# Weight parts lent to GpSimd in the mixing projections, with the turn between two blocks and a routing in another order

## The chip, the cores and the metric

The kernel runs on one core of a Trainium2 chip. A core has a matrix engine (TensorE; in the profile PE, its weight loads PEld), a vector engine (VectorE, DVE), an activation engine (ScalarE, ACT), GpSimd (POOL) and a queue that issues the transfers (SyncE, SP). They run side by side, each takes its own instructions in a fixed order, and semaphores tell one when another is done. The metric is the device time of one execution in microseconds, the median of several.

## The reference

One sequence of 256 tokens with 1024 channels goes through two blocks, all in float32. The first has two layers; in each:

```python
x = x + 0.5 * swiglu_ffn(rms_norm(x, ffn1_norm_g[l]), ffn1_w_in[l], ffn1_w_out[l])
proj = rms_norm(x, mix_norm_g[l]) @ w_mix_in[l]          # 1024 x 3328
...   # 8 heads of a delta-rule recurrence (rwkv7) from 1792 columns, 8 heads of attention from 1536
x = x + concatenate([y_rwkv, y_moba]) @ w_mix_out[l]
x = x + memory_cross_attention(...)                       # 256 tokens of a memory
x = x + 0.5 * swiglu_ffn(...)
```

A norm closes it. The second block computes six rows of modulation from a condition vector `c` (`c @ w_ada + b_ada`: shift, scale and gate, twice), and then:

```python
h = rmsnorm(x, norm1_w) * (1 + scale1) + shift1
proj = h @ w_in            # a chunked mLSTM, a differential attention, gates
x = x + gate1 * (merged @ w_out)
h2 = rmsnorm(x, norm2_w) * (1 + scale2) + shift2
# logits of 4 groups and 32 experts: h2 @ w_rg + b_rg, h2 @ w_re + b_re
# top group, top 2 of its 8 experts; each expert is a swiglu of width 256
x = x + gate2 * sum over experts of combine[:, e] * (silu(h2 @ w_gate[e]) * (h2 @ w_up[e])) @ w_down[e]
```

## The kernel before, in words

**A product.** The weights lie in main memory as units of 128 partitions x 2048 columns, read as two halves of 128 x 1024 (`raw`, 512 KB each). PE multiplies in a reduced float32 form, so each operand is cut into two parts: ACT rounds a half to `wh`, DVE subtracts, `wl = raw - wh` (`parts`, L534). The activations have parts too, `XH` and `XL`. `mm3` (L568) then issues three products into one accumulation in PSUM: `XH wh`, `XH wl`, `XL wh`. A half of a projection of 512 columns has four such triples.

**What is prepared when.** `prefetch` (L556) keeps halves ahead in the order of a fixed stream: in the mixing stage `wh` and `wl` have two buffers each, so the parts of a half are written while the half before it is multiplied; the feed-forward stages lend a third buffer, the second block has five. `raw` has four. A list `behind` names instructions; the parts that are made next are put behind them on their engine (`issue_after`).

**The order of the work.** Each stage is a set of generators (`mix`, `proj`, `rwkv_early`, `lora` and so on). `Weave` picks the next by priority and by due times from a planner of its own (`Clock`, L252), which has costs for every engine's operations, GpSimd's too. The order in which instructions come out is the order of each engine's queue, as far as the framework does not move them.

**The mixing stage** (`mix`, L865) multiplies 13 units a layer: unit 0 the low-rank inputs, 1 to 6 the columns of the recurrence in the order in which the heads need them, 7 to 12 the attention's. Between the products run the heads: DVE builds decays and keys with scans and element-wise operations (`rwkv_early`, L955), PE and DVE solve a triangular system (`rwkv_chunk`, `rwkv_solve`), GpSimd computes powers for the norms and a few products of 256 or 512 columns.

**The turn.** `final_norm` (L1509) waits for the last feed-forward, sums the squares of `x` and of `x` times the gain (ACT, eight calls; DVE multiplies by the gain), and GpSimd computes the power `r`. `block2` (L1939) then calls `prep_modulated` (L733): for each half of the channels DVE scales two token tiles by `rr`, PE transposes them into PSUM, ACT and DVE apply scale and shift, and `split` makes `XH` and `XL`. After the first two scalings two halves of weights are made. `settle` (L1543) scales `x` itself on GpSimd.

**The routing.** `route_weights` (L2035), spawned at lowest priority in the middle of the second block, loads the 288 columns of router weights and the bias, multiplies shift by the weights on PE (eight products) for the bias, and scales and splits the weights. `route` (L2055) multiplies `h2` by them (two accumulating passes in each of eight blocks; the second half waits for the second half of `X`), makes logits, takes the first largest group, counts places with three small products, and `places` makes the permutation with which `pick` gathers the tokens of each expert group.

Of the kernel before, what the change touches and what calls it, by code (L numbers as in the profile page):

```python
# [19 lines left out]
P = 128  # L20
D = 1024
KT = 8
# [425 lines left out]
class Prog:  # L448
    def __init__(self, ctx, tc, a):
        self.clock = Clock()  # L450
        self.tc, self.nc, self.a = tc, Timed(tc.nc, self.clock), a
        nc = self.nc
        pool = lambda name, **k: ctx.enter_context(tc.tile_pool(name=name, **k))
        self.cp = pool("cst", bufs=1)
        self.wp = pool("wts", bufs=2)
        self.ap_ = pool("act", bufs=2)
        self.pp = pool("psum", bufs=2, space=PSUM)
        self.dp = pool("dram", bufs=1, space=DRAM)
        self.uid = 0
        self.turn = {}  # L460
        self.weave = Weave(self.clock)
        self.spawn = self.weave.add
        self.order, self.loads, self.ahead = stream(), collections.deque(), collections.deque()
        self.chunks, self.mod = collections.deque(), None
        self.version, self.uses = [1, 1], 0
        self.sp, self.spare = None, {}
        self.behind, self.stop = [], None
        self.loan = {}

# [4 lines left out]
    def ps(self, tag):  # L474
        n = BANKS[tag]
        return self.tile(self.pp, [P, 512], F32, tag, tag, n)

# [56 lines left out]
    def parts(self, raw):  # L534
        h, l = self.wtile("wh", F32R), self.wtile("wl", F32R)
        with ExitStack() as later:
            for z in self.behind:
                later.enter_context(self.tc.issue_after(z.ins))
            quiet, self.clock.quiet = self.clock.quiet, True
            self.nc.scalar.activation(h, raw, AF.Copy)  # L540
            self.nc.vector.tensor_sub(l, raw, h.bitcast(F32))
            self.clock.quiet = quiet
        return h, l

    def weights(self, name, j, i, n=99):

        self.prefetch(n)
        u, w = self.ahead.popleft()
        assert u == (name, j, i), (u, name, j, i)
        return w  # L550

# [4 lines left out]
    def prefetch(self, n=99):  # L556
        while len(self.ahead) < min(n, self.lookahead("wh")):
# [5 lines left out]
            self.ahead.append((u, self.parts(raw)))  # L563
# [4 lines left out]
    def mm3(self, out, xh, xl, wh, wl, start, stop):  # L568
# [3 lines left out]
        mm(out, xl, wh, start=False, stop=stop)  # L572
# [26 lines left out]
    def setup(self):  # L599
# [31 lines left out]
        self.modc = self.cp.tile([P, 48], F32, name="modc")  # L631
        self.gates = self.dp.tile([2, 8, P], F32, name="gates")

    def setup_later(self):

        yield 0, 12.0
        self.nc.sync.dma_start(self.csts[:, P:], self.a["cst"][:, P:])
        self.setup2()
        yield 0, 20.0
        self.setup_bias()  # L640
# [92 lines left out]
    def prep_modulated(self, gain, shift):  # L733
# [3 lines left out]
        for hf in range(2):  # L737
            xn = []
            for t in range(2):
                xn.append(self.k("s2", 512))  # L740
                z = nc.vector.tensor_scalar(xn[t], self.x[t][:, hf * 512:hf * 512 + 512], self.rr[:, t:t + 1], None, op0=OP.mult)
            if hf == 0:
                self.behind, self.stop = [z, *self.behind], None
                self.prefetch(2)
            for k in range(0, 4, 2):
# [15 lines left out]
                self.behind = self.split(pair.H[:, sl], pair.L[:, sl], tg.rearrange("p (k t) -> p k t", k=2))  # L761
# [747 lines left out]
    def final_norm(self):  # L1509
# [11 lines left out]
        def squares(i, hf):  # L1521
            for t, x in enumerate(self.halves(self.x)):
                j = 4 * i + 2 * hf + t
                sq = nc.scalar.activation(self.k("s2", 512), x[hf], AF.Square, accum_out=ss[:, j:j + 1])
# [18 lines left out]
    def settle(self):  # L1543

        r = self.rsqrt(self.rf, 2, 1.0 / D, EPS)
        for t in range(2):
            self.nc.gpsimd.tensor_scalar(self.x[t], self.x[t], r[:, t:t + 1], None, op0=OP.mult)
# [100 lines left out]
    def modulation(self, l):  # L1648

        sc = self.sp.tile([P, 8], F32, name=f"sc{l}")  # L1650
# [288 lines left out]
    def block2(self):  # L1939
# [4 lines left out]
        self.bident, self.bmask = (self.cst(n).bitcast(BF16) for n in ("bid", "bmask"))  # L1944
        X = yield from self.prep_modulated(*self.modulation(0))
# [89 lines left out]
    def route_weights(self):  # L2035

        nc = self.nc
        self.sc, self.shift = self.modulation(1)
        w = self.k("wrt", 288)
        nc.sync.dma_start(w, self.a["wrt"])  # L2040
        b = self.row("brt", "brt", 36)
        yield 0, self.due(w)
        o = self.ps("tr")
        for k in range(KT):
            nc.tensor.matmul(o[:, :36], self.shift[:, k:k + 1].to_broadcast([P, P]), w[:, k * 36:(k + 1) * 36],
                             start=k == 0, stop=k == KT - 1)
        self.brow = self.sp.tile([P, 36], F32, name="brow")
        nc.vector.tensor_tensor(self.brow, o[:, :36], b, op=OP.add)
        v = w.rearrange("p (k n) -> p k n", n=36)
        nc.vector.tensor_tensor(v, v, self.sc[:, :, None].to_broadcast([P, KT, 36]), op=OP.mult)  # L2050
        self.wr = self.sp.tile([P, KT, 72], F32R, name="wr")
        self.split(self.wr[:, :, :36], self.wr[:, :, 36:], v)
        yield 1.7, 0

    def route(self, X, N):  # L2055
# [6 lines left out]
        for k in range(KT):  # L2062
            if k == 4:
                yield lambda: X.ok[1]
            if k:
# [14 lines left out]
        for t in range(2):  # L2080
            stt(lg[:, t], o[:, t * 36:(t + 1) * 36], X.r[:, t:t + 1], self.brow, op0=OP.mult, op1=OP.add)
        oh = t2(self.k("oh", 8))
# [9 lines left out]
        tt(far, o[:, :8], self.cst("end"), op=OP.is_gt)  # L2092
        stt(pl, far, -10000.0, o[:, :8], op0=OP.mult, op1=OP.add)
# [248 lines left out]
    def beyond(self, state, out):  # L2342
# [13 lines left out]
        with self.tc.If(most > P):  # L2356
# [10 lines left out]
            for e in range(8):  # L2367
# [16 lines left out]
             m64=8, qkw=1, sg=8, ss=2, wrt=1, brt=1)  # L2384
# [66 lines left out]
```

## Time and profile before

| | us |
|---|---|
| median of three runs | 1953.47 (1950.83 to 1955.53) |
| the profiled execution | 1955.89 |
| its span, first to last instruction | 1954.0 |

| engine | busy us | share |
|---|---|---|
| PE | 1895.5 | 97% |
| DVE | 1403.3 | 72% |
| ACT | 1060.4 | 54% |
| POOL | 73.6 | 4% |

The profile is of one execution. Busy time of PE is modelled at the ends of the products, which overlap, so a row's length on PE is longer than its distance to the next row; the starts are exact. A float32 product that is not in the reduced form stands as two records. The granted clock (PEclk) is 1.00 at 2.4 GHz and 0.50 at 1.2 GHz. In a timeline row the bracket says how long the engine had been idle and what ended that.

### The profile page before, as it was taken

What the parts mean: (1) busy time and instruction counts of PE and PEld (TensorE: products, weight loads), DVE (VectorE), ACT (ScalarE), POOL (GpSimd) and SP (SyncE); (2) the same over time, 40 slices, a digit from 0 to 9 for tenths busy, and PEclk for the clock granted to TensorE, in tenths of its full rate; (3) what the DMA queues carried; (4) which work ended last, traced back from release to release, by engine and by line L of the source; (5) the groups of instructions that cost most, each with busy time, mean ns of one, the idle gap of its engine ahead of it and who ended that gap; (6) DMA issues with size and microseconds to landing.
All of it is one profiled execution on the core that took longest, in us unless ns stands there. A gap on an engine that the chain in (4) does not pass through costs nothing.

```text
span 1954.0 us, 26240 instructions
## 1 busy us (share of the span) xinstructions
PE 1895.5 (97%) x9524; PEld 1536.3 (79%) x9524; DVE 1403.3 (72%) x2287; ACT 1060.4 (54%) x1608; POOL 73.6 (4%) x67
## 2 busy tenths in 40 slices
PE   8999999999999999999999999999899998999997
PEld 6888778888788878888777888888687777877775
DVE  6766787664666676666877655666787677999897
ACT  4444654655544444445536655444555546777674
POOL 0000011000000000000110000000011000000000
PEclk9999999999999999999999999999999998999999
DMA  8766442244567656665314353676564453999996
GB/s 276 246 224 225 127 127 69 89 157 151 172 212 228 210 203 218 223 214 170 126 41 126 98 191 115 221 221 212 189 203 140 141 174 138 337 342 363 328 337 220
DMA packets 114806, 381.41 MB, mean 195 GB/s; under 512 B 17080, under 2 KB 21864, under 8 KB 114544
## 3 DMA queue, kind: packets, MB, share of 16 engines
q1 hardware_dynamic: 114672, 379.68, 58.6%
q8 instruction: 77, 1.26, 0.3%
q14 instruction: 57, 0.47, 0.1%
HBM read 378.03 MB, written 3.17 MB: 195 GB/s over the span
## 4 chain that ended last, share of the span: by engine, by line
PE 75%; issue 11%; DVE 8%; ACT 2%; DMA 1%; POOL 1%; SPq 0%; DVEq 0%; POOLq 0%; ACTq 0%
PE mm L378 39%; PE acc L378 31%; PE tr L378 5%; DVE wl L378 3%; ACT wh L378 1%; POOL rs L378 1%; DVE s L378 1%; DVE el L378 1%; DMA raw<-in_w_dram 1%; DVE t1k L378 0%; ACT s L378 0%; DVE AR L378 0%; DVE XL L378 0%; DMA K<-in_mem_dram 0%; DMA x<-in_x_dram 0%
## 5 line engine op out<-in xcount | busy, mean ns | idle before, releaser
L378 DVE TENSOR_TENSOR wl<-raw,wh 128x1024 fp32r<-128x1024 f32 x648 | 785.9, 1225 | 326.8 <-ACT wh L378 324.3
L378 ACT ACTIVATE wh<-raw 128x1024 fp32r<-128x1024 f32 x648 | 676.0, 1057 | 526.2 <-PE mm L378 301.6
L378 PE MATMUL mm<-wh,XH 128*128 128x512 f32 (+1 forms) x1456 | 578.6, 399 | 4.1 <-ACT s L378 2.5
L378 PE MATMUL mm<-wl,XH 128*128 128x512 f32 (+1 forms) x1456 | 573.0, 394 | 2.6 <-DVE wl L378 2.0
L378 PE MATMUL mm<-wh,XL 128*128 128x512 f32 (+1 forms) x1456 | 571.1, 392 | 0.3
L378 PEld LDWEIGHTS mm<-wl,XH 128*128 128x128 f32 x1456 | 274.5, 189 | 65.0 <-DVE wl L378 10.6
L378 PEld LDWEIGHTS mm<-wh,XH 128*128 128x128 f32 x1456 | 274.9, 189 | 63.3 <-ACT s L378 3.8
L378 PEld LDWEIGHTS mm<-wh,XL 128*128 128x128 f32 x1456 | 274.3, 189 | 57.7 <-DVE XL L378 1.1
L378 PE MATMUL acc<-wh,X 128*128 128x512 f32 x352 | 142.9, 406 | 0.0
L378 PE MATMUL acc<-wh,T 128*128 128x512 f32 x352 | 139.1, 395 | 0.0
L378 PE MATMUL acc<-wl,X 128*128 128x512 f32 x352 | 139.1, 395 | 0.0
L378 PE MATMUL acc<-wl,XH 128*128 128x512 f32 x288 | 114.7, 398 | 3.0 <-DVE wl L378 2.8
L378 PE MATMUL acc<-wh,XH 128*128 128x512 f32 x288 | 114.4, 404 | 0.9 <-ACT XH L378 0.5
L378 PE MATMUL acc<-wh,XL 128*128 128x512 f32 x288 | 113.5, 395 | 0.0
L378 PE MATMUL acc<-wh,ah 128*128 128x512 f32 x256 | 85.9, 396 | 1.2 <-ACT ah L378 1.2
L378 DVE SCALAR_TENSOR_TENSOR el<-raw,vecs,el 128x512 f32<-128x512 f32 x84 | 63.1, 751 | 31.0 <-DMA raw<-in_w_dram 29.3
L378 PEld LDWEIGHTS acc<-wh,T 128*128 128x128 f32 x352 | 66.3, 188 | 15.8
L378 PEld LDWEIGHTS acc<-wl,X 128*128 128x128 f32 x352 | 66.4, 189 | 13.8
L378 PEld LDWEIGHTS acc<-wh,X 128*128 128x128 f32 x352 | 66.3, 188 | 13.4
L378 POOL TENSOR_TENSOR rs<-s,emh 128x2 f32<-128x2 f32 (+2 forms) x28 | 31.5, 1128 | 1150.6 <-DVE s L378 1143.3
L378 PEld LDWEIGHTS acc<-wl,XH 128*128 128x128 f32 x288 | 54.8, 190 | 18.1 <-DVE wl L378 7.6
L378 ACT ACTIVATE t1k<-mm,rh 128x256 f32<-128x256 f32 x80 | 37.9, 474 | 49.0 <-PE mm L378 49.0
(368 smaller groups left out, 2082.0 us busy)
## 6 DMA issues: line engine op xcount, KB each, us to landing
raw<-in_w_dram SPq DMA_DIRECT2D x696, 512.0 KB
ext<-ext SPq DMA_DIRECT2D x1, 2048.0 KB
K<-in_mem_dram SPq DMA_DIRECT2D x8, 256.0 KB
x<-in_x_dram SPq DMA_DIRECT2D x4, 256.0 KB
bi<-ext SPq DMA_DIRECT2D x4, 256.0 KB
sm<-ext SPq DMA_DIRECT2D x4, 256.0 KB
w<-gates SPq DMA_DIRECT2D x2, 512.0 KB
out_dram<-x SPq DMA_DIRECT2D x4, 256.0 KB
```

The costliest lines, as they stand in the source:

```text
L378: r = f(*args, **kw)
```

## The change

Three groups of edits. In the mixing stage, for units 3 and up, the subtraction of every second half is issued on GpSimd. At the turn one half of weights is made ahead of the transposes and the others behind the splits of the tiles; the second half's scaling and `x` itself go to GpSimd with a second multiplication by 1.0 in the instruction; the last square goes to DVE; the router's bias products go right behind the last product of the first block. In the routing PE gets dummy products whose result nobody reads, each waiting for an operand of the routing; the router's weights and bias are loaded at the start of the kernel into tiles of their own.

```diff
+    def busy(self, n, gate, cols=512):
+        m = math.prod(gate.shape[1:])
+        for _ in range(n):
+            self.nc.tensor.matmul(self.ps("tr")[:m, :cols], gate, self.start[:, :cols], start=True, stop=True)
...
-    def parts(self, raw):
+    def parts(self, raw, pool=False):
...
-            self.nc.vector.tensor_sub(l, raw, h.bitcast(F32))
+            (self.nc.gpsimd if pool else self.nc.vector).tensor_tensor(l, raw, h.bitcast(F32), op=OP.subtract)
...
+    def lent(self, name, j, i):
+        return i == 1 and name[:3] == "mix" and j >= 3
...
-            self.ahead.append((u, self.parts(raw)))
+            self.ahead.append((u, self.parts(raw, self.lent(*u))))
...
-        mm(out, xl, wh, start=False, stop=stop)
+        self.tail = mm(out, xl, wh, start=False, stop=stop)
...
     def setup_later(self):
...
+        self.nc.sync.dma_start(self.wrt, self.a["wrt"])
+        self.nc.sync.dma_start(self.brt, self.a["row"][0:1, ROW.sl("brt")].to_broadcast([P, 36]))
...
     def prep_modulated(self, gain, shift):
...
-                z = nc.vector.tensor_scalar(xn[t], self.x[t][:, hf * 512:hf * 512 + 512], self.rr[:, t:t + 1], None, op0=OP.mult)
-            if hf == 0:
-                self.behind, self.stop = [z, *self.behind], None
-                self.prefetch(2)
+                xs = self.x[t][:, hf * 512:hf * 512 + 512]
+                if hf:
+                    z = nc.gpsimd.tensor_scalar(xn[t], xs, self.rr[:, t:t + 1], 1.0, op0=OP.mult, op1=OP.mult)
+                else:
+                    z = nc.vector.tensor_scalar(xn[t], xs, self.rr[:, t:t + 1], None, op0=OP.mult)
+            self.scaled = self.scaled or z
...
-                self.behind = self.split(pair.H[:, sl], pair.L[:, sl], tg.rearrange("p (k t) -> p k t", k=2))
+                high, low = self.split(pair.H[:, sl], pair.L[:, sl], tg.rearrange("p (k t) -> p k t", k=2))
+                if hf == 0:
+                    self.behind = [low, *self.behind[-1:]]
+                    self.prefetch(2 + k // 2)
+                else:
+                    self.behind = [high, low]
...
         def squares(i, hf):
             for t, x in enumerate(self.halves(self.x)):
                 j = 4 * i + 2 * hf + t
+                if i == hf == t == 1:
+                    nc.vector.scalar_tensor_tensor(self.k("s2", 512), x[hf], 1.0, x[hf], op0=OP.mult, op1=OP.mult,
+                                                   accum_out=ss[:, j:j + 1])
+                    break
...
-            self.nc.gpsimd.tensor_scalar(self.x[t], self.x[t], r[:, t:t + 1], None, op0=OP.mult)
+            self.nc.gpsimd.tensor_scalar(self.x[t], self.x[t], r[:, t:t + 1], 1.0, op0=OP.mult, op1=OP.mult)
...
     def block2(self):
...
+        self.stop = None
+        self.prefetch(1)
+        self.spawn(self.route_bias(), 5)
+        yield 0, 0
         X = yield from self.prep_modulated(*self.modulation(0))
...
     def route_weights(self):
...
+        with self.tc.issue_after(self.scaled.ins):
+            self.sc, _ = self.modulation(1)
+            nc.vector.tensor_tensor(v, v, self.sc[:, :, None].to_broadcast([P, KT, 36]), op=OP.mult)
...
+    def route_bias(self):
...
+        o = self.ps("tr")
+        with self.tc.issue_after(self.tail.ins):
+            for k in range(KT):
+                nc.tensor.matmul(o[:, :36], self.shift[:, k:k + 1].to_broadcast([P, P]), self.wrt[:, k * 36:(k + 1) * 36],
+                                 start=k == 0, stop=k == KT - 1)
+        yield lambda: self.scaled
+        self.brow = self.cp.tile([P, 36], F32, name="brow")
+        with self.tc.issue_after(self.scaled.ins):
+            nc.vector.tensor_tensor(self.brow, o[:, :36], self.brt, op=OP.add)
...
     def route(self, X, N):
...
                 yield lambda: X.ok[1]
+                for _ in range(4):
+                    mm(self.ps("tr"), X.H[:, 4, :P], X.H[:, 0:2], start=True, stop=True)
...
+        self.busy(1, lg[:, 0])
...
         tt(far, o[:, :8], self.cst("end"), op=OP.is_gt)
+        self.busy(2, far)
```

## Rows read from the trace of the kernel before

**Rows 1.** The page's busy line: busy us (share of the span) xinstructions.
```profile
PE 1895.5 (97%) x9524; PEld 1536.3 (79%) x9524; DVE 1403.3 (72%) x2287; ACT 1060.4 (54%) x1608; POOL 73.6 (4%) x67
```

**Rows 2.** Windows, both mixing stretches: length, each engine's busy us, PEclk, DMA share, GB/s.
```profile
222.00:345.00 123.00, 115.30 (x752) 93.62 (x751) 97.92 (x242) 64.63 (x117) 20.07 (x16) 0.97 0.33 103
921.00:1045.00 124.00, 115.47 (x747) 93.85 (x745) 97.77 (x239) 63.33 (x116) 19.99 (x16) 0.97 0.31 100
```

**Rows 3.** The page's groups, the weight parts: busy us, mean ns, idle before, releaser.
```profile
L378 DVE TENSOR_TENSOR wl<-raw,wh 128x1024 fp32r<-128x1024 f32 x648 | 785.9, 1225 | 326.8 <-ACT wh L378 324.3
```

**Rows 4.** Groups by form on POOL, the two largest element-wise shapes.
```profile
L378 POOL TENSOR_SCALAR x<-x,rs 128x1024 f32<-128x1024 f32 x2 | 6.6, 3318 | 0.1
...
L378 POOL TENSOR_TENSOR rkv<-rkv,el 128x512 f32<-128x512 f32 x4 | 5.1, 1270 | 7.3 <-DVE AR L378 7.3
```

**Rows 5.** Timelines of POOL and DVE, twice side by side: start, us, instruction.
```profile
242.00 3.21 POOL L378 TENSOR_TENSOR bkh<-BK,pe 128x256 f32<-128x256 f32 x1 [6.87 <-DVE BK L378]
...
242.18 2.35 DVE L378 TENSOR_TENSOR wl<-raw,wh 128x1024 fp32r<-128x1024 f32 x2
...
338.85 0.63 POOL L378 TENSOR_TENSOR t1k<-csts,pe 128x256 f32<-128x256 f32 x1 [0.16 <-DVE W L378]
...
338.93 1.63 DVE L378 TENSOR_TENSOR wl<-raw,wh 128x1024 fp32r<-128x1024 f32 x1
```

**Rows 6.** Timeline, the parts of halves (3,1) and (12,1) and their first products.
```profile
226.21 1.23 DVE L378 TENSOR_TENSOR wl<-raw,wh 128x1024 fp32r<-128x1024 f32 x1 [2.02 <-ACT wh L378]
...
228.18 0.39 PE L378 MATMUL mm<-wl,XH 128*128 128x512 f32 x1
...
336.00 1.21 DVE L378 TENSOR_TENSOR wl<-raw,wh 128x1024 fp32r<-128x1024 f32 x1
...
337.58 0.39 PE L378 MATMUL mm<-wl,XH 128*128 128x512 f32 x1
```

**Rows 7.** Timeline of PE, first mixing stretch, its longest wait before 250 us.
```profile
249.98 0.30 PE L378 MATMUL tr<-csts,rkv 128*128 128x128 f32 x1 [1.52 <-DVE rkv L378]
```

**Rows 8.** Timelines of PE, POOL and DVE at the turn; last two: windows.
```profile
1406.92 0.40 PE L378 MATMUL acc<-wh,T 128*128 128x512 f32 x1
1412.99 1.94 PE L378 MATMUL tr<-csts,s 128*128 128x128 f32 x8 [5.67 <-ACT wh L378]
1416.34 1.21 PE L378 MATMUL tr<-csts,s 128*128 128x128 f32 x4 [1.41 <-DVE s L378]
...
1417.55 0.63 PE L378 MATMUL mm<-wh,XH 128*128 128x512 f32 x1
...
1411.38 0.69 POOL L378 TENSOR_TENSOR r<-s,emh 128x2 f32<-128x2 f32 x1 [186.48 <-DVE s L378]
...
1412.99 2.35 DVE L378 TENSOR_TENSOR wl<-raw,wh 128x1024 fp32r<-128x1024 f32 x2
1415.26 0.54 DVE L378 TENSOR_SCALAR s<-tr,sc,modc 128x256 f32<-128x256 f32 x1
...
1409.80:1419.90 10.10, 5.50 (x21) 4.47 (x22) 7.68 (x18) 8.40 (x16) 2.47 (x3) 0.50 0.60 182
1416.60:1419.90 3.30, 3.30 (x13) 2.72 (x13) 2.55 (x6) 2.17 (x5) 1.78 (x2) 0.50 0.79 291
```

**Rows 9.** Timelines of PE and SP: the router's bias products and weight load.
```profile
1517.19 1.87 PE L378 MATMUL tr<-wrt,modc 128*128 128x36 f32 x16
...
1416.69 0.43 SPq L378 DMA_DIRECT2D wrt<-in_wrt_dram  x1
```

**Rows 10.** Window and PE's timeline of the routing; last, float32 products elsewhere.
```profile
1631.70:1641.80 10.10, 7.76 (x34) 7.60 (x35) 8.22 (x32) 6.89 (x14) 0.00 (x0) 0.50 0.01 2
...
1632.83 1.86 PE L378 MATMUL tr<-oh,csts 128*128 128x8 f32 x8 [1.39 <-DVE oh L378]
1635.91 4.61 PE L378 MATMUL acc<-pr,y 128*128 128x256 f32 x20 [1.22 <-DVE pr L378]
...
477.97 1.89 PE L378 MATMUL acc<-pt,rkv 128*128 128x256 f32 x8
```

More of the change, by code (lines that the diff above doesn't have):

```diff
@@ L468, in __init__ @@
         self.loan = {}
+        self.tail = self.scaled = None
     def nm(self, s):
@@ L631, in setup @@
         self.modc = self.cp.tile([P, 48], F32, name="modc")
+        self.wrt = self.cp.tile([P, 288], F32, name="wrt")
+        self.brt = self.cp.tile([P, 36], F32, name="brt")
         self.gates = self.dp.tile([2, 8, P], F32, name="gates")
@@ L1648, in modulation @@
     def modulation(self, l):
-        sc = self.sp.tile([P, 8], F32, name=f"sc{l}")
+        sc = self.cp.tile([P, 8], F32, name=f"sc{l}")
         self.nc.vector.scalar_tensor_tensor(sc, self.modc[:, 24 * l + 8:24 * l + 16], 1.0, self.vec(f"n{l + 1}"),
@@ L2037, in route_weights @@
         nc = self.nc
[L2038 to L2048, printed above, removed]
+        w = self.wrt
         v = w.rearrange("p (k n) -> p k n", n=36)
-        nc.vector.tensor_tensor(v, v, self.sc[:, :, None].to_broadcast([P, KT, 36]), op=OP.mult)
+        with self.tc.issue_after(self.scaled.ins):
+            self.sc, _ = self.modulation(1)
+            nc.vector.tensor_tensor(v, v, self.sc[:, :, None].to_broadcast([P, KT, 36]), op=OP.mult)
         self.wr = self.sp.tile([P, KT, 72], F32R, name="wr")
         self.split(self.wr[:, :, :36], self.wr[:, :, 36:], v)
+        yield 0, 0
+    def route_bias(self):
+        nc = self.nc
+        self.shift = self.modc[:, 24:32]
+        o = self.ps("tr")
[7 more added lines that the diff above has]
+            nc.vector.tensor_tensor(self.brow, o[:, :36], self.brt, op=OP.add)
         yield 1.7, 0
@@ L2383 @@
 BUFS2 = dict(s8=16, rs=6, rh=4, s16=4, w4=3, t1k=4, s2=8, qk=4, vm=4, wif=2, lf=2, og=2, wrow=2, nmx=2, F=6, E=4, PT=4,
-             m64=8, qkw=1, sg=8, ss=2, wrt=1, brt=1)
+             m64=8, qkw=1, sg=8, ss=2)
 SPARE = dict(raw=0, wh=3, wl=3)
```

## The prediction

> **What bounds the kernel now.** I read the busy line first: TensorE (PE) is busy 97% of the span [rows 1]. So a change pays only where PE stands still, runs at half clock, or has work moved into time in which it stood. The table by stages says where: in the two mixing stretches PE is busy 115.3 of 123 us and 115.5 of 124 us [rows 2], and at the turn between the blocks and at the routing the granted clock is halved for some ten microseconds each, as parts B and C show. Then the groups: all 648 second weight parts (`wl`, raw minus the rounded first part) are made on VectorE (DVE) at 1225 ns each [rows 3]. The timelines of the three stretches give the rest.
>
> **Part A, lending.** `lent` picks halves i = 1 of units 3 to 12, 10 per layer, 20 in all. Removed from DVE: 20 x 1.22 = 24.5 us, no PE time by itself. Added to GpSimd (POOL): 20 subtractions of 128x1024, a size the trace does not have there. The nearest is 128x512 with two inputs in 1270 ns [rows 4]; 128x256 takes 0.63 us [rows 5], so each further 256 columns cost 0.64 us and 1024 come to 1.27 + 2 x 0.64 = 2.55 us (an estimate). The one other 1024-column row on POOL, a multiplication, takes 3318 ns [rows 4]; ends 2.5 and 3.3, I take 2.55, the same operation.
>
> Is it late for PE? Only two buffers of each part exist in this stage, so a half is prepared while the half before it is multiplied. Three lent halves of the first layer have no room [rows 6]: the part of (3,1) starts at 226.21 and its first product at 228.18; (12,1): 336.00 and 337.58. With 2.55 us they end at 228.76 and 338.55, late by 0.58 and 0.97 us. For (7,1) I read the same distance as for (3,1), some 0.5 us. The other seven have over a microsecond of room by the same comparison. PE executes in order, so this is +2.1 us a layer.
>
> What does DVE's relief give back? PE stands 1.52 us before the transposes at 249.98, waiting for DVE [rows 7], and the part of (5,1) is the second of the two in 242.18 [rows 5], ahead of DVE's work for that wait. Taking it away is worth its 1.2 us: -1.2 us a layer. Elsewhere in the stretch PE has other work or waits for a chain through several engines; zero.
>
> The price of company: POOL and DVE shut each other out. POOL's 128x256 operation at 242.00 took 3.21 us beside two DVE parts, five times the 0.63; the other way, the DVE part at 338.93 took 1.63 us beside that POOL operation, where the mean is 1.225 [rows 3, 5]. So each lent part can stop DVE for up to 2.55 us to save it 1.22, a net loss of 1.33 us, or be starved itself. About five of ten lie beside DVE's long runs from SBUF ((4,1), (5,1), (7,1), (8,1), (9,1), by the timeline). Bounds of A per layer: nothing late and both relief and another wait of that size gone, -3.0; all late and all five blockings on PE's path, 2.1 + 5 x 1.33 = +8.8. Between ends this far apart I take the terms that have rows: 2.1 - 1.2 = +0.9, **+1.8 us** for two layers. Also queued behind a waiting lent part on POOL are the powers for the normalisations, which the chains of the heads need; that is part of the same upper bound.
>
> The Trainium skill (SBUF — State Buffer, "Who interferes with whom") states that the pair of ports that VectorE shares with GpSimd is held for a whole instruction, that a VectorE operation with two SBUF inputs contends for it with GpSimd's reads, and that the loser blocks fully. The two pairs of rows agree in both directions. By that rule alone every lent part that meets such an operation costs DVE more than it frees, and the change loses; this is rival 2 below.
>
> **Part B, the turn.** Now PE's last product starts at 1406.92, the first transposes come at 1412.99, the first product of the second block at 1417.55, and the clock is at 0.50 from 1409.8 to 1419.9 [rows 8]. Three things move.
> First, the eight products of the routing bias (16 records) take 1.87 us at 1517.19 in the middle of PE's work [rows 9]; they go right behind the last product of the first block, into idle time. -1.9 us. What they need (weights, modulation) must be there: the two small loads go from SP's queue in the turn (0.43 us of issue each [rows 9]) to the start of the kernel, where the queue has room; I cost it at nothing, 0.9 us if a weight load waits behind them there.
> Second, DVE makes two weight parts in 1412.99 to 1415.34, and the scaling of the first transposed tile, which the first product needs, comes only at 1415.26 [rows 8]. After the change one part is made before the power's result is back, the others behind the split of each tile. The gain is at most the 2.35 us, at least nothing, if the part in front delays the scaled rows instead or if the bias's PSUM bank holds back the second transposes. Half: -1.1 us. The second half's scaling goes to POOL: 128x512 at half of 3318 ns, 1.7 us each [rows 4], 3.3 in all from the end of the power at 1412.1, so 1415.4, before the 1416.34 of the next transposes now [rows 8]; hidden unless POOL keeps DVE's own two scalings out, then +1.7.
> Third, the clock. It fell when PE had stood since 1407.3. With 1.9 us of products in that gap it may fall later or rise sooner; half clock costs PE 3.3 us of work in 1416.6 to 1419.9 [rows 8], half of it is loss. I take -0.9 of at most -1.7. The last square, moved from ACT to DVE, is one 128x512 operation in front of the same four small ones either way; zero, plus or minus 0.2.
> Sum B: **-3.9 us**, bounds -6 and +1.5.
>
> **Part C, the routing.** The clock is at 0.50 from 1631.7 to 1641.8; eight records take 1.86 us there, then twenty take 4.61 us [rows 10]. The change gives PE dummy products in the waits: four of 128x512 before the second half's routing products, one behind the logits, two behind the group test. If the clock holds, 6.5 us of work shrinks by up to 3.2; part of that PE would then spend waiting for DVE's and ACT's splits of the gathered columns. Gain 2.5, at most 4. If it does not hold, the dummies themselves stand in the way: eight records (four float32 products of 256 columns) take 1.89 us at full clock [rows 10], so one of 512 columns takes about 0.9, at half clock 1.8, and two behind the group test at 1634.1 end at 1637.7 where the gathering now starts at 1635.91: +1.8, and the one before it +0.6. I take the clock as held: **-2.5 us**, bounds -4 and +2.4.
>
> **Sum.** 1.8 - 3.9 - 2.5 = -4.6 us against the profiled execution, 1955.89 us (span 1954.0), so 1951.3 there. That execution lies 2.4 us above the median 1953.47, so I predict **1949 us** for the median. After the routing the loads run close to their limit, but they start when the first expert's buffers come free, so an earlier routing moves them too.
>
> **Rivals.** *1. Lending pays as well:* DVE's relief closes PE's waits in the mixing stretches, A at its good end of -6, with B and C as above: 1941. For it: PE is idle 7.7 and 8.5 us there [rows 2] and the waits I looked at end on DVE. Against: several also pass through ACT and PE itself.
> *2. The shared ports decide:* lent parts stop DVE's chains for the heads, and DVE stops POOL so that more parts come late. From the point where four of the five blockings in each layer reach PE's path, A is 2 x (2.1 + 4 x 1.33 - 1.2) = +12.4; with B and C at -6.4 that is +6.0: 1959. For it: the 3.21 and 1.63 [rows 5]. Against: much of DVE's work there reads PSUM, and PE has weight products to run meanwhile.
> *3. The clock is not held:* it falls at the turn and the routing as before and the dummies cost; B gives -1.9 - 1.1 = -3.0, C +2.4, A +1.8: +1.2, 1955. For it: PE still waits about 4 us for the norm at the turn. Against: the gaps of the routing are at most 1.4 us and each gets a filler.
>
> **How the numbers follow.** The forecast 0.45, rival 1 0.15, rival 2 0.20, rival 3 0.20. What can be told from no change here is 0.2%, 3.9 us, so faster means under 1949.6. The forecast lies on that edge with its own spread towards the gain: I give it 0.31 faster, 0.14 same; with rival 1 faster is 0.46. Rival 2 gives 0.18 slower and 0.02 same; rival 3 0.12 same, 0.08 slower (when a dummy and a lent part both delay): same 0.28, slower 0.26. The range reaches from just below rival 1 to rival 2, 1940 to 1959; the forecast's own is 1944 to 1954.
>
> **What would show it.** A: POOL subtractions of 128x1024 near 2.6 us; PE waiting for `wl` before the first products of (3,1), (7,1), (12,1); the wait before the rkv transposes down from 1.5 to 0.3 us. If lent parts last 4 us or DVE's operations beside them 2 us, rival 2 is on. B: eight bias products at the end of the first block, first product 1 us sooner after PE's last. C: granted clock 1.00 through the routing and the twenty gathering records in some 2.5 us. It would be wrong if the mixing stretches change by more than 5 us each, or the clock falls in both places as before.

## The result, and the profile after

The changed kernel takes 1985.12 us (median of 5, 1980.92 to 1988.16), the kernel before beside it 1954.72 (1950.83 to 1955.53): a ratio of 1.0155, 95% interval 1.0142 to 1.0168. The prediction was 1949, its range ended at 1959.

Where the time went is read from one mark per stage, the start of ScalarE's cast of the stage's first half, after minus before (us):

| stage that begins | mark before | shift |
|---|---|---|
| first mixing | 198.46 | +0.30 |
| feed-forward behind it | 514.77 | +18.24 |
| second mixing | 895.11 | +17.42 |
| feed-forward behind it | 1213.85 | +32.92 |
| second block, unit 8 | 1457.71 | +32.52 |
| experts | 1613.40 | +29.48 |

The two mixing stages took 17.9 and 15.5 us more, together 33.4. The stretch from there to unit 8, with the turn in it, gave back 0.4 and the second block 3.0. (The profiled execution is the slowest of the five, 1988.16 us; from the last mark to its end it lost another 2.8.)

The page of the changed kernel, its busy line and the products with `wl` (busy us, mean ns, idle before them and its releaser):

```profile
PE 1912.4 (96%) x9534; PEld 1534.7 (77%) x9534; DVE 1406.2 (71%) x2267; ACT 1060.1 (53%) x1606; POOL 121.8 (6%) x89
...
L378 PE MATMUL mm<-wl,XH 128*128 128x512 f32 (+1 forms) x1456 | 578.6, 397 | 13.1 <-POOL wl L378 7.6
```

DVE lost twenty subtractions and is busier than before [rows 1]: that is the first sign. The mixing stretches, in the columns of [rows 2], with their ends moved by the shifts:

```profile
222.00:362.40 140.40, 124.33 (x781) 98.27 (x780) 100.28 (x232) 64.59 (x117) 43.68 (x26) 0.96 0.30 95
938.40:1077.00 138.60, 123.01 (x777) 96.85 (x777) 99.38 (x227) 63.47 (x116) 43.80 (x26) 0.96 0.28 91
```

POOL works 24 us more in each, DVE not one less. The granted clock is the smaller part: it stood at 0.50 for 13.7 us in each of the two mixing stages, for 6.8 us in each before. Half of the difference, 3.4 us a stage, is my estimate of what that can have cost. The lent parts by form on POOL, busy us and mean ns:

```profile
L378 POOL TENSOR_TENSOR wl<-raw,wh 128x1024 fp32r<-128x1024 f32 x20 | 49.1, 2455 | 80.4 <-ACT wh L378 75.2 <-issue 5.3
```

2455 ns: the estimate of 2.55 us was right. Two of them in the timeline of the changed kernel:

```profile
238.27 2.40 POOL L378 TENSOR_TENSOR wl<-raw,wh 128x1024 fp32r<-128x1024 f32 x1 [2.63 <-issue]
238.34 2.60 DVE L378 TENSOR_TENSOR AR<-rkv,el 128x256 f32<-128x256 f32 x1
240.72 0.50 PE L378 MATMUL mm<-wl,XH 128*128 128x512 f32 x1 [1.43 <-POOL wl L378]
...
329.19 2.35 POOL L378 TENSOR_TENSOR wl<-raw,wh 128x1024 fp32r<-128x1024 f32 x1
329.25 2.57 DVE L378 TENSOR_TENSOR YL<-YL,rs 128x256 f32<-128x256 f32 x1 [0.19 <-POOL rs L378]
331.88 0.44 PE L378 MATMUL tr<-csts,YL 128*128 128x128 f32 x2 [2.04 <-DVE YL L378]
```

In both pairs a DVE operation that takes 0.42 us elsewhere starts 0.07 us behind POOL's and ends 0.28 us behind POOL's end; PE then waits 2.04 us for the second. That is rival 2. But the time for which DVE's operations were held beside lent parts (those over 0.4 us beyond the median of their form without lending) sums to only 11.7 us in the first stretch, not all on the path to PE, and PE's instructions stand in another order: of the 1848 of the first mixing stage at least 278 moved. (Another count, which the expectations below use, gives 458 of some 1350.)

The turn of the changed kernel, last product of the first block to first of the second, with POOL's powers and scalings and the DVE part beside them:

```profile
1439.01 0.40 PE L378 MATMUL acc<-wh,T 128*128 128x512 f32 x1
...
1443.34 1.23 DVE L378 TENSOR_TENSOR wl<-raw,wh 128x1024 fp32r<-128x1024 f32 x1
...
1443.51 1.61 POOL L378 TENSOR_TENSOR r<-s,emh 128x2 f32<-128x2 f32 x1 [185.96 <-DVE s L378]
...
1445.86 2.00 PE L378 MATMUL tr<-csts,s 128*128 128x128 f32 x8 [4.74 <-issue]
...
1446.53 0.81 POOL L378 TENSOR_TENSOR rs<-s,emh 128x2 f32<-128x2 f32 x1 [1.40 <-DVE sc L378]
1447.33 1.56 POOL L378 TENSOR_SCALAR s<-x,r 128x512 f32<-128x512 f32 x2
...
1448.93 1.94 PE L378 MATMUL tr<-csts,s 128*128 128x128 f32 x8 [1.07 <-POOL s L378]
1450.52 0.78 PE L378 MATMUL mm<-wh,XH 128*128 128x512 f32 x1
```

From the last product to the first it is 11.51 us, 10.63 before [rows 8]. The power takes 1.61 us beside the part that was made ahead of time, 0.69 alone. In POOL's queue the power for `x` itself (`rs`) stands ahead of the two scalings; it waits 1.40 us for DVE, and PE waits 1.07 us for the scaled rows.

### The profile page after: what moved, and what is told of

It reads as the page before. It is cut to its first block, busy times and chain, and to the rows that moved or that the text cites. A ratio compares the mean times of both kernels' runs of the same rounds, so it can differ in the third digit from the quotient of the medians.

```text
span 1986.3 us, 26250 instructions
## 1 busy us (share of the span) xinstructions
PE 1912.4 (96%) x9534; PEld 1534.7 (77%) x9534; DVE 1406.2 (71%) x2267; ACT 1060.1 (53%) x1606; POOL 121.8 (6%) x89
## 5 line engine op out<-in xcount | busy, mean ns | idle before, releaser
L378 DVE TENSOR_TENSOR wl<-raw,wh 128x1024 fp32r<-128x1024 f32 x628 | 759.7, 1221 | 333.0 <-ACT wh L378 331.1
L378 PE MATMUL mm<-wl,XH 128*128 128x512 f32 (+1 forms) x1456 | 578.6, 397 | 13.1 <-POOL wl L378 7.6
```

The lines of the kernel that those rows point to most:

```text
L378: r = f(*args, **kw)
```

## The experiments

Each is compared with the kernel before on the same chip: the ratio stands behind the median, its 95% interval in brackets. The kernel before took 1950.9 to 1954.2 us from group to group, so a difference between two groups is uncertain by some 3 us.

**One part at a time.** e1 takes the lending out of the changed kernel, e4 the routing's dummies as well.

```diff
     def lent(self, name, j, i):
-        return i == 1 and name[:3] == "mix" and j >= 3
+        return False
```

> The changed kernel with lent() returning False: VectorE makes every second part, all other edits stay. In the two mixing stretches the instructions of TensorE stand in the order of the kernel before. If lending alone costs the time (the comparison of the two traces puts about 17.9 and 15.5 us of loss into the two mixing stretches), this kernel loses those 33 us and lands at about 1985 - 33 = 1952, 1 to 4 us under the kernel before. If the turn and the routing carry part of the loss, it stays above 1958. My prediction's sum for those two parts alone was -6.4 us, about 1948.

Measured: 1952.34 us, ratio 0.9987 (0.9978 to 0.9996). The lending costs 1985.1 - 1952.3 = 33 us; the rest of the change gains 1.8 us by the medians, 0.8 to 4.3 by the interval. PE, ACT and DVE have the order of the kernel before in both mixing stages.

```diff
-                for _ in range(4):
-                    mm(self.ps("tr"), X.H[:, 4, :P], X.H[:, 0:2], start=True, stop=True)
...
-        self.busy(1, lg[:, 0])
...
-        self.busy(2, far)
```

> The kernel without lending, and the routing's seven dummy products left out as well; what remains of the change is the turn and the bias products. The difference to the kernel without lending is the worth of the dummies. If they hold the clock as predicted they are worth 2.5 us and this one is that much slower; if the clock falls anyway (the changed kernel's trace shows 0.50 for 6.8 us at the routing, before 10.2) they are worth 0 to 1.5 us.

Measured: 1952.04, 0.9993 (0.9984 to 1.0002). The dummies are worth nothing that can be measured. The profiles are of two kinds. In e1's timeline of PE the two behind the group test run at half clock and stand in the way, then the gathering is short:

```profile
1631.07 3.58 PE L378 MATMUL tr<-start,oh 128*8 128x512 f32 x4 [0.26 <-DVE oh L378]
1634.58 2.56 PE L378 MATMUL acc<-pr,y 128*128 128x256 f32 x20
```

Before, the gathering started at 1635.91 [rows 10]; e1 is 3.47 us ahead at the last mark in front of the routing, so it would have started at 1632.44. It starts 2.1 us later and takes 2.05 less. In the traces of e5, e8 and e12 below, with the same dummies, the granted clock is 1.00 through the whole routing. Here e12:

```profile
1631.64 1.88 PE L378 MATMUL tr<-start,oh 128*8 128x512 f32 x4 [0.26 <-DVE oh L378]
1633.46 2.56 PE L378 MATMUL acc<-pr,y 128*128 128x256 f32 x20
```

There ScalarE's casts of the weights behind the routing come 1.8 us sooner, measured from the last mark in front of it. In e5 and e12 this is lost again within some 20 us, where the clock now stands at 0.50 for 6.8 us (3.4 before); in e8 it stays.

**Plan or chip.** The lending changes two things: who subtracts, and what the planner believes (2.37 us on POOL's time line for 1.225 on DVE's). e2 (its edit is shown) tells the planner the old price; e3 leaves the work on DVE and tells it the new one.

```diff
-            (self.nc.gpsimd if pool else self.nc.vector).tensor_tensor(l, raw, h.bitcast(F32), op=OP.subtract)
+            args = (l, raw, h.bitcast(F32))
+            getattr(self.tc.nc, "gpsimd" if pool else "vector").tensor_tensor(*args, op=OP.subtract)
+            self.clock.note("DVE" if pool else "DVE", "tensor_tensor", args, {})
```

> The lent parts are still subtracted on GpSimd, but the planner is told that they cost what they cost on VectorE. The order on TensorE is then close to that of the kernel before (56 of some 1350 instructions of the first mixing stretch moved, against 458 in the changed kernel). Theory 'order' (the planner's higher price for GpSimd re-weaves the stage, and fillers are spent early, so that the second head's chain runs bare): most of the loss goes, 1956 to 1963. Theory 'engine' (parts of 2.4 us come late on TensorE, and the shared ports stop VectorE): the loss stays, 1975 to 1990.

> The reverse: VectorE makes all parts at 1.22 us, but the planner is told GpSimd's price for every second one. The order on TensorE is then close to that of the changed kernel (429 of some 1350 moved against the kernel before). Theory 'order': the loss stays although GpSimd does nothing more, 1970 to 1985. Theory 'engine': it goes, 1950 to 1958.

Measured: e2 1970.53, 1.0088 (1.0073 to 1.0104); e3 1977.23, 1.0119 (1.0104 to 1.0135). e2 lies between the two ranges, e3 in that of 'order'. Both theories are half right: each half costs 18 to 25 us without the other.

In both, some instructions still stood in another order than in the kernel whose order was meant. e5 and e6 tie every instruction of PE, ACT and DVE of the first block behind its predecessor in the order of e1 (e5, POOL subtracts) or of the changed kernel (e6, DVE subtracts); the lent parts alone are free. The traces show these orders to be the same, instruction by instruction, in both mixing stages.

```diff
             w.finish(w.add(first(), 10))
+            pin(tc)
```

> As the run in which GpSimd makes the lent parts under the old plan, but every instruction of TensorE, ScalarE and VectorE in the first block is tied behind the one that precedes it in the kernel without lending: the orders of the three engines are identical to that kernel's (1952.3), the twenty subtractions alone have moved to GpSimd's queue. What is left is what the chip does with them. Theory 'it was all order' (56 instructions had still moved in the run before): 1953 to 1957. Theory 'the chip's part is real' (late parts, shut-out VectorE, and the clock that falls behind longer waits): the loss stays, 1963 to 1972. The waits before products with wl sum to about 2 us a layer in that run's trace, so lateness alone gives 1956 to 1958.

> The reverse: VectorE makes every part in 1.22 us, and TensorE, ScalarE and VectorE keep exactly the order of the changed kernel in the first block. Theory 'the order is bad by itself': 1974 to 1982, as in the run with the new plan on VectorE (1977.2). Theory 'the order was only bad because parts were late': 1952 to 1960.

Measured: e5 1969.41, 1.0081 (1.0063 to 1.0099); e6 1971.84, 1.0093 (1.0072 to 1.0114), a little under the range given for a bad order.

| us | old order | new order |
|---|---|---|
| DVE subtracts | 1952.3 (e1) | 1971.8 (e6) |
| POOL subtracts | 1969.4 (e5) | 1985.1 (changed) |

So 17 us are the chip's, 19.5 the order's, and together they cost 33, a little less than their sum. The clock explains neither: it stood at 0.50 for 10.2 us in the two mixing stages of e5 and for 13.6 in those of e6, as in those of e1 (13.6).

**What the chip's part is.** In e5's timeline the same pairing, at a small step of the triangular solve (`W`) and at a product of 512 columns (`Y`):

```profile
264.87 2.39 POOL L552 TENSOR_TENSOR wl<-raw,wh 128x1024 fp32r<-128x1024 f32 x1 [6.27 <-ACT wh L381]
...
265.87 1.48 DVE L381 TENSOR_TENSOR W<-W,t1k 32x72 f32<-32x72 f32 x1
...
282.59 2.97 POOL L552 TENSOR_TENSOR wl<-raw,wh 128x1024 fp32r<-128x1024 f32 x1 [0.81 <-POOL t1k L381]
...
283.33 2.78 DVE L381 TENSOR_TENSOR Y<-c,csts 128x512 f32<-128x512 f32 x1
...
288.36 1.97 PE L381 MATMUL tr<-csts,Y 128*128 128x128 f32 x8 [4.71 <-DVE el L381]
```

In e1, where the order is the same:

```profile
280.44 0.67 DVE L378 TENSOR_TENSOR Y<-c,csts 128x512 f32<-128x512 f32 x1
...
283.36 1.97 PE L378 MATMUL tr<-csts,Y 128*128 128x128 f32 x8 [1.54 <-DVE el L378]
```

2.78 for 0.67 us, and PE's wait grows from 1.54 to 4.71. The relief that the prediction counted on is lost in the same way. In e5, beside the part of (5,1), whose removal was to shorten PE's wait at 249.98 [rows 7]:

```profile
245.03 2.51 POOL L552 TENSOR_TENSOR wl<-raw,wh 128x1024 fp32r<-128x1024 f32 x1
...
245.20 2.37 DVE L381 TENSOR_SCALAR AR<-el 128x2 f32<-128x2 f32 x1
...
251.90 0.30 PE L381 MATMUL tr<-csts,rkv 128*128 128x128 f32 x1 [1.79 <-DVE rkv L381]
```

DVE is rid of 1.22 us and held for 2.2, and PE waits 1.79 us instead of 1.52. In the first mixing stage seven of the ten parts hold a DVE operation for over a microsecond. Summed over DVE's operations held by more than 0.4 us beside POOL, the time above each form's median in e1 is 15.8 us in e5 and 2.1 in e1, for the first layer: 13.7 us lost for the 12.25 (10 x 1.225) saved. The sum alone isn't the price. What was held lies on chains that PE waits for: PE's idle time in this stage grows from 9.1 to 16.0 us, and by the marks the stage takes 7.0 us more. Late parts are the lesser share: the idle time before products with `wl`, both layers, is 2.6 us in e1, 6.0 in e5. e7 was to show the company alone: DVE keeps all its parts and POOL makes the ten again for nobody.

```diff
-            (self.nc.gpsimd if pool else self.nc.vector).tensor_tensor(l, raw, h.bitcast(F32), op=OP.subtract)
+            self.nc.vector.tensor_tensor(l, raw, h.bitcast(F32), op=OP.subtract)
+            if pool:
+                self.tc.nc.gpsimd.tensor_tensor(self.k("sm", 1024), raw, h.bitcast(F32), op=OP.subtract)
```

> The kernel without lending, all orders identical to it, and GpSimd makes the ten subtractions of each layer a second time into a tile that nobody reads. TensorE never waits for them, so no part is late; what they can cost is the company: VectorE shut out while GpSimd holds the shared port, GpSimd shut out by VectorE, and its powers for the norms queued behind. Theory 'company': most of the loss of the run with the same order is here too, 1960 to 1970. Theory 'lateness': nothing, 1951 to 1955.

Measured: 1992.56, 1.0202 (1.0183 to 1.022): 40 us, far above the range of either theory and more than the real lending. DVE pays here and is not relieved, and POOL's powers queue behind the subtractions; how the 40 us divide was not measured. Its timeline shows both directions, and a power of 128x8 queued behind:

```profile
277.30 2.39 POOL L553 TENSOR_TENSOR sm<-raw,wh 128x1024 f32<-128x1024 f32 x1 [4.48 <-ACT wh L381]
...
277.56 2.25 DVE L381 TENSOR_TENSOR t1k<-W 32x112 f32<-32x112 f32 x1
279.63 2.82 POOL L381 TENSOR_TENSOR s<-s,emh 128x8 f32<-128x8 f32 x1
279.74 1.21 DVE L381 TENSOR_TENSOR wl<-raw,wh 128x1024 fp32r<-128x1024 f32 x1
```

e9 and e10 split the ten by what stood beside them in e5, with the orders tied as there; e10 lends the other seven.

```diff
-        return i == 1 and name[:3] == "mix" and j >= 3
+        return i == 1 and name[:3] == "mix" and j in (3, 4, 6)
```

> Only the halves (3,1), (4,1) and (6,1) of each layer are lent, the three beside which no operation of VectorE was held up in the run with all ten and the same order; orders tied as there. Theory 'company' (a lent part costs what it holds up on VectorE): 0.35 us of late part for (3,1) per layer at most, 1952 to 1954.5. Theory 'every lent part costs its share' (lateness, the fixed cost of GpSimd): three tenths of 17 us, 1957 to 1958.

> The other seven halves are lent, the same orders. Theory 'company': all the loss of the ten, 1966 to 1971. Theory 'every lent part costs its share': seven tenths of 17 us, 1964.

Measured: three lent 1952.84, 0.9993 (0.9983 to 1.0003), no loss against e1; seven lent 1972.77, 1.0098 (1.0081 to 1.0115), all of it (1966 to 1971 was expected). In e9, beside a lent part of the same length, DVE's operations read PSUM (`tr`) and keep their 0.48 us, and PE's wait for the late part is 0.36:

```profile
225.76 2.39 POOL L552 TENSOR_TENSOR wl<-raw,wh 128x1024 fp32r<-128x1024 f32 x1 [13.47 <-ACT wh L381]
226.36 0.48 DVE L381 SCALAR_TENSOR_TENSOR rkv<-tr,omu,sh 128x256 f32<-128x256 f32 x1 [2.66 <-ACT sh L381]
...
228.21 0.50 PE L381 MATMUL mm<-wl,XH 128*128 128x512 f32 x1 [0.36 <-POOL wl L552]
```

The twenty lent parts of e5 sort DVE's operations in the same way. Of those that began with at least half a microsecond of the lent part to go, the 16 that read PSUM took at most 0.02 us longer than the median of their form in e1, and two reductions of 128x512 in SBUF 0.03. All 14 others were held, by 1.25 to 2.2 us: twelve with two SBUF inputs, and two `TENSOR_SCALAR` of 128x2 that read one tile in SBUF (the 2.37 us above).

e11 makes each lent part in four pieces.

```diff
...
+            for c in range(0, 1024, 256 if pool else 1024):
+                s = slice(c, c + (256 if pool else 1024))
+                getattr(self.tc.nc, "gpsimd" if pool else "vector").tensor_tensor(*(z[:, s] for z in args), op=OP.subtract)
```

> All ten lent with the same orders, each subtraction as four of 256 columns on GpSimd. If VectorE is shut out until an instruction of GpSimd ends, it now waits for some 0.6 us instead of up to 2.4, and the loss falls to 4 to 10 us, 1956 to 1962, with the parts themselves later because VectorE gets in between. If what counts is how long GpSimd works, or the lateness, nothing changes or it grows, 1968 to 1975.

Measured: 1963.88, 1.0056 (1.0039 to 1.0073): 11.5 us above e1 for 17, between the two ranges. DVE now gets in between the pieces, 0.3 to 0.45 us late each time (the same steps take 0.22 alone):

```profile
264.06 2.83 POOL L554 TENSOR_TENSOR wl<-raw,wh 128x256 fp32r<-128x256 f32 x4 [5.86 <-ACT wh L381]
...
265.09 0.49 DVE L381 TENSOR_TENSOR W<-W,t1k 32x72 f32<-32x72 f32 x1
...
265.62 0.67 DVE L381 TENSOR_TENSOR t1k<-W 32x88 f32<-32x88 f32 x1
266.32 0.67 DVE L381 TENSOR_TENSOR W<-W,t1k 32x88 f32<-32x88 f32 x1
```

The single wait follows the length of the instruction on POOL; the loss falls by less, as there are more waits (23 held operations in the first layer for e5's 12) and POOL needs longer for the four.

**What the order's part is.** The planner now believes two things, that DVE is free of the parts and that they come later. In e13 and e14 DVE makes all parts, the order is not tied, and the planner holds one belief each (e13: the parts on POOL's time line at 1.225 us; e14: DVE charged as well, and the part ready after POOL's 2.37). In e15 (its edit is shown) POOL makes them, and the planner holds DVE as well until the part is done.

```diff
...
+            getattr(self.tc.nc, "gpsimd" if pool else "vector").tensor_tensor(*args, op=OP.subtract)
+            self.clock.note("POOL" if pool else "DVE", "tensor_tensor", args, {})
+            if pool:
+                self.clock.at["DVE"] = max(self.clock.at["DVE"], self.clock.at["POOL"])
```

> VectorE makes all parts. The planner puts the twenty parts on GpSimd's time line at VectorE's price (1.225 us), so it believes VectorE free of them and no part late. 202 of some 1350 instructions of TensorE in the first mixing stretch move against the kernel without lending, and the order is near the one with GpSimd's full price (59 differ). Theory 'belief in relief' (the planner pulls the heads' chains forward to times that VectorE doesn't keep): the loss stays, 1968 to 1980. Theory 'belief in late parts': most of it goes, 1952 to 1960.

> VectorE makes all parts and the planner keeps it charged for them, but counts each of the twenty parts as ready only after GpSimd's 2.37 us. 230 of 1350 move. Theory 'belief in relief': little of the loss, 1952 to 1960. Theory 'belief in late parts': most of it, 1968 to 1980.

> GpSimd makes the twenty parts, and the planner charges GpSimd its 2.37 us and holds VectorE as well until the part is done, which is near what the traces show. If a planner with the right model finds an order that suits, the loss falls below that of the old order (1969.4): 1958 to 1967. If every order other than the old one is worse, or the chains simply lack the time that the port takes, 1969 to 1985.

Measured: e13 1973.26, 1.0105 (1.0089 to 1.0122); e14 1964.58, 1.006 (1.0043 to 1.0076); e15 1971.46, 1.0098 (1.0081 to 1.0115). The belief in relief costs 21 us by itself, the belief in late parts 12 (e13 lies in the range of its theory, e14 between the two), and the planner that holds both engines does no better than the old order (e5). In the order of the changed kernel, which e6 keeps with DVE making the parts, products wait for parts. The page's line for them in e1, and in e6:

```profile
L378 PE MATMUL mm<-wl,XH 128*128 128x512 f32 (+1 forms) x1456 | 573.7, 394 | 2.6 <-DVE wl L378 2.2
```

```profile
L381 PE MATMUL mm<-wl,XH 128*128 128x512 f32 (+1 forms) x1456 | 576.3, 396 | 11.2 <-DVE wl L552 10.4
```

That is 8.6 us more of idle time, of the 19.5. In e13 this line has 5.3 us, and by the marks all of the 9.3 us that it loses in the first layer arise behind 339 us of e1; in e6 5.2 of 8.6 have arisen by then.

The relief moves one thing that can be seen in e3, e6, e13 and the changed kernel: the second head's solve is issued ahead of the transposes of the memory. PE in e1, and in e13:

```profile
341.23 1.04 PE L378 MATMUL tr<-csts,K 128*128 128x128 f32 x8
...
350.58 2.14 PE L378 MATMUL acc<-X,A 128*128 128x128 f32 x16
```

```profile
344.64 0.63 PE L378 MATMUL tr<-csts,Y 128*128 128x128 f32 x4 [2.63 <-DVE Y L378]
345.96 1.65 PE L378 MATMUL acc<-X,A 128*128 128x128 f32 x6 [0.69 <-ACT X L378]
...
367.84 0.66 PE L378 MATMUL tr<-csts,K 128*128 128x128 f32 x4
```

The memory's weight products need these transposes: between 350 and 367 PE has 31 weight products in e1 and none in e13. Is that the cause? Three runs hold the second head until the memory is prepared.

```diff
-        C.append(self.spawn(self.rwkv_late(l, 1, lo, E1, R1, V1, Y, [E1, kv], C), 1))
+        C.append(self.spawn(self.rwkv_late(l, 1, lo, E1, R1, V1, Y, [E1, kv, lambda: self.mem == l], C), 1))
...
+        self.mem = l
```

> The run with the belief in relief (VectorE makes all parts, 1973.3), with the second head held until the memory is prepared. Theory 'missing filler' (the memory's weight products are not there when the second head's chain waits): most of the 20 us go, 1953 to 1960. If the loss lies elsewhere in the new order (first head, wl behind other work): 1966 to 1975.

> The changed kernel itself (GpSimd makes the parts under its own price) with the same hold. Theory 'missing filler': it comes down from 1985 to what the ports alone cost, 1966 to 1972. If the two causes are not separate: 1975 to 1985.

> Control: the kernel without lending with the same hold (227 of 1350 instructions move). If the hold is free, 1950 to 1955; if it costs by itself (the second head starts later than it could), that is what the two runs beside it carry too.

Measured: e16 1982.47, 1.0158 (1.0141 to 1.0175); e17 2001.01, 1.0247 (1.023 to 1.0264); e18 1985.29, 1.017 (1.0153 to 1.0187). The control itself lost 34 us against the kernel before on its chip: the second head's solve starts at 383 instead of 351, and PE waits at its end for 4.55, 1.00 and 1.30 us with no other products between. So my theory got no test of a repair. The differences do say something: with the second head fixed in that place the belief in relief costs nothing (e16 against e18, -2.8), and lending costs 15.7 (e17 against e18), near the 17 of e5. That fits a price of the relief that lies in where the second head stands, but doesn't show it: the hold is so dear that it may hide the rest, and in e16 only 50 of PE's 1848 instructions stand otherwise than in e18. Of the order's 19.5 us 8.6 are waits for parts (e6); what makes the others stays open.

**Turn and GpSimd's form.** e8 is e1 with the early part behind the two scalings, and the router's scaling behind the turn's last split.

```diff
+            if hf == 0:
+                self.behind = [z, *self.behind]
+                self.prefetch(1)
...
+                    self.late = low
...
-        self.prefetch(1)
         self.spawn(self.route_bias(), 5)
...
-        with self.tc.issue_after(self.scaled.ins):
+        with self.tc.issue_after(self.late.ins):
             self.sc, _ = self.modulation(1)
```

> The kernel without lending with two repairs at the turn. Its trace shows the early weight part on VectorE (1409.64, 1.23 us) beside GpSimd's power, which took 1.61 us where it takes 0.69 before; the part now goes behind the two scalings. And the scaling of the router weights with its split stands in VectorE's queue ahead of the first tile's scaling (1412.4 to 1414.6, with 0.74 us of waiting for ScalarE); it now goes behind the last split of the turn. Theory 'these two stand on the path': 0.9 us for the power and 0.5 to 1.2 us for the queue, so 1950 to 1951 against 1952.3. If the first product waits for something else (the clock, the weights' transfers), no difference.

Measured: 1951.81, 0.9990 (0.9981 to 0.9999), the fastest of all, though not told from e1. The power is back at 0.70 us, but last product to first is 11.25 us (e1 11.51): the second transposes wait 0.33 us for the bias's PSUM bank, which DVE frees only behind the part, and those of the second half 0.65 and 0.19 us for POOL's scalings.

e12 takes the multiplication by 1.0 out of POOL's scalings.

> The kernel without lending, with the second multiplication by 1.0 taken out of the scalings at the turn, which GpSimd makes. In the kernel before, 128x1024 with one multiplication took 3.3 us; without lending, with two, the pair of 128x1024 takes 3.7 in all and the pair of 128x512 1.55. If the form makes the difference, the pairs take about 6.6 and 3.3 us here; if it was the company of VectorE, they stay at 3.7 and 1.55.

Measured: 1952.53 in one run. The groups of POOL by form, with one multiplication (e12) and with two (e1):

```profile
L378 POOL TENSOR_SCALAR x<-x,rs 128x1024 f32<-128x1024 f32 x2 | 7.0, 3486 | 0.0
L378 POOL TENSOR_SCALAR s<-x,r 128x512 f32<-128x512 f32 x2 | 3.1, 1565 | 0.0
```

```profile
L378 POOL TENSOR_SCALAR x<-x,rs 128x1024 f32<-128x1024 f32 x2 | 3.7, 1860 | 0.0
L378 POOL TENSOR_SCALAR s<-x,r 128x512 f32<-128x512 f32 x2 | 1.6, 785 | 0.0
```

The form makes the difference: the second operation halves the time. It need not be all: in e8 the 128x1024 with two multiplications took 2628 ns, for a reason that stays open.

## Why the prediction was wrong

**Part A failed, and it alone decides: +1.8 predicted, +33 measured.** Three steps.
- "Between ends this far apart I take the terms that have rows: 2.1 - 1.2." The lateness had its row, and e5 puts it at 3.4 us for both layers (predicted 4.2); in the changed kernel's own order the waits before these products grow by 10.5 us (13.1 against e1's 2.6), 7.6 of them for POOL's parts. The company had rows too, the 3.21 and 1.63 of [rows 5], and I priced it at zero. I looked for DVE's long runs near five of the parts; what counts is the next DVE operation without a PSUM operand (a reduction apart), and the triangular solve is one small SBUF operation after the other. Seven of ten were hit. The rule that I weighed there is that of the Trainium skill (SBUF — State Buffer, "Who interferes with whom"): a shared pair of ports, held for the whole instruction, the loser blocked. It agrees with these runs: the held DVE operations end within 0.6 us of POOL's end, a quarter of the length leaves 0.49 to 0.67 us where e5 has 1.48 to 2.78, and the operations that read PSUM in e9 are not held.
- The relief in the same sum, -1.2 us a layer, did not come: with the order unchanged PE's wait before the rkv transposes is 1.79 us (e5), 1.52 before. The next DVE operation was held for 2.2 us where the part had taken 1.22.
- Removed from DVE: "24.5 us, no PE time by itself". No term of my sum had the planner in it, though its prices, GpSimd's too, make the order. Both beliefs that the lending gives it cost time with DVE doing the same work as before (12 and 21 us). The order's 19.5 and the chip's 17 together lie outside my upper bound of +8.8 a layer (16.7 measured). That bound held only for an unchanged order (8.5 a layer in e5).

**Rival 2** had the mechanism and, with four blockings a layer, 12.4 us; the same-order run gives 17. It was short of the result by the order's part.

**Part B: -3.9 predicted; without lending the first product comes 0.9 us later, not 1 sooner.** The 1.9 us of the bias products did go from the second block, which is 3.0 us shorter by the marks of e1 too; where the other 1.1 come from isn't shown. The gain at the turn did not come: the part made ahead is itself company for POOL's power (1.61 us for 0.69), the split of the router weights stood in DVE's queue ahead of the first tile, and in e8, where these two are gone, the bank of the bias holds the second transposes, the doubt that stood in the text. The scalings on POOL were shorter than priced, 1.55 us for 3.3, but not hidden as I took them to be: another power stands ahead of them in POOL's queue, and PE waits 1.07 us for them.

**Part C: -2.5 predicted, nothing measured.** The clock was half right: 0.83 over the ten microseconds in e1's profile, 1.00 in those of e5, e8 and e12, where [rows 10] has 0.50. Where it fell, the price of a dummy that stands in the way and the gain of a fast gathering cancel to 0.1 us. Where it held, 1.8 us came, against the 2.5 of the sum, and were lost again in two of the three: my sum ended at the routing and had no term for a clock that falls behind it instead.

Parts B and C gave -1.8 us by the medians of e1, where -6.4 was expected.

## What to carry to other kernels

Before lending work to GpSimd, list for each lent instruction the VectorE operation that will run beside it: if it reads SBUF alone, charge up to the whole length of the lent instruction to VectorE, and if the chain hangs on it, to the kernel (reductions were the exception here). Where a planner writes the order, a change of engine is two changes; measure each with the other held fixed, by tying the order. Work placed in a wait is not free if the wait ends on an engine that it keeps company.

## What was not expected of the hardware

- On GpSimd a scaling with a second multiplication by 1.0 takes 1860 ns for 128x1024 and 785 for 128x512; with one multiplication 3486 and 1565.
- A VectorE operation of 128x2 elements with one input in SBUF took 2.37 us beside a lent part, 0.16 alone; operations that read PSUM took no more than alone.
- A power of 128x8 on GpSimd took 2.82 us beside a VectorE subtraction of 1024 columns, where it takes 1.64 (2.73 already in the kernel before, beside such a part), and one of 128x2 1.61 us, where it takes 0.69.
- Four subtractions of 128x256 on GpSimd took 852 ns each on the mean, 3.4 us for what takes 2.46 in one piece, and still cost less (11.5 us against 17).
